# Picks transposed some steps later, and two weight splits held behind the second norm's scaling

## The chip, the cores and the metric

One core of a Trainium2 chip. The metric is the device time of one execution in microseconds; less is better.

## The reference

One decoder block on x of 256 tokens x 1024 (batch 1), all in float32. It has two residual steps. In the first, RMSNorm(x) times one wide matrix gives the inputs of an attention branch (16 heads, here one causal block of 256 keys) and of a Mamba-2 branch (convolution, scan, gated norm); both are projected to 1024, gated, summed and multiplied by `w_out`. The second is a retrieval of experts, cut here to what matters:

```
xn = rms_norm(x, norm2_g)
q  = (xn @ w_q).reshape(T, 8, 256)
s1 = einsum('thd,hkd->thk', q[..., :128], keys1)
s2 = einsum('thd,hkd->thk', q[..., 128:], keys2)
v1, i1 = top_k(s1, 16)
v2, i2 = top_k(s2, 16)
sv, pos = top_k(v1[..., :, None] + v2[..., None, :], 16)
eidx = take_along_axis(i1 * 128 + i2, pos)
gw = softmax(sv)
act = einsum('td,thkd->thk', xn, u_tab[eidx])
x = x + einsum('thk,thkd->td', gelu(act) * gw, v_tab[eidx])
```

## The kernel before

**Weights.** All weights pass through one stream of 392 pieces of 128 x 1024 float32: 88 of the input projection, 24 of the two branch projections, 8 of `w_out` (112 to 119), 16 of `w_q` (120 to 135), 128 of `u_tab` and 128 of `v_tab`. A piece is loaded on SP's queue (L107, a ring `wr` of three buffers) and split into two float32r parts, `wh` by an ACT copy (L120, ring of four) and `wl` = raw - `wh` by a subtraction (ring of four) on DVE (L128), or, for about a third of the pieces, on POOL (L125). `ahead()` (L110) keeps loads five and splits three pieces ahead of the one in use; `state["cap"]` limits the splits. Every product is three matmuls: high x high, high x low, low x high.

**Order.** The kernel is written as a main line of matmuls, with the small work as Python generators in `active`. `tick()` (L141) advances each of them by one `yield`. In `product_T` (L155) and `u_pair` (L906) a tick comes after every 12 matmuls, in `product_half` (L177) after every 12 too. The framework then orders the instructions of each engine itself, by its own estimated costs and the program's order as priority, so an engine's order can differ from the written one. `tc.issue_after(ins)` makes what is issued within it follow `ins` on the same engine. `tc.keep_in_program_order` does so for the engine's previous instruction. Each engine runs its queue in order.

**Second norm.** After the input stage the out projection makes four blocks `b` of 256 columns into the PSUM tiles `pO` (L730 to L741). For blocks 2 and 3 it makes the first token half (`tt` = 0), appends `norm2(0)`, and then the second half with `norm2(1)`. `norm2` (L721) adds the residual into `xt` (L713), sums squares (L718), adds them (L724), takes the root on POOL (`rn`, L198), scales `xt` into `xn` (L238, two instructions of 512 columns), has `xn` transposed on TensorE (L243), and ACT and DVE make `xh` (L250) and `xl` (L251) of it. `psq0` (L743) is the first block of the queries: its first token half needs `xh` and `xl` of the first half alone. Its weights are pieces 120 and 121. Piece 120's `wl` is a DVE subtraction, piece 121's a POOL one; those of 122 and 123 are already put behind the last `xh` and `xl` (L118). Before the change the splits of 120 and 121 are issued while the weights of blocks 2 and 3 are fetched.

**Picks.** `topk(tt)` (L811) finds the 16 experts of 8 heads for one token half in 61 steps on DVE: top 16 of the scores, of the candidates, softmax weights, then for each of two key halves a one-hot over ranks that yields the index `so` (L864 to L881). The step after the second `so` transposes both `so` and the weights `gt` on TensorE into the PSUM tile `ptk` (L885), and the next step copies them to `selT` (ACT, L887) and `g2` (DVE, L890 to L892). `picks` (L959) chains topk(0) and topk(1), and `paced` puts each step's DVE work behind the last `wl`.

**u_tab and gates.** `u_pair` (L906) multiplies xn with two pieces of `u_tab` in 48 matmuls. After the pair in which `picks` ends, `start` is set (L969), the pool of the picks is closed, and `one_hots` (L929) and `gate_group` (L942) of 8 tokens each follow over the remaining pairs: with n = 62 - `start`, pair k after it has the groups from 32k/n to 32(k+1)/n. Then the `v_tab` stage makes the output.

Of the kernel before, what the change touches and what calls it, by code (L numbers as in the profile page):

```python
# [15 lines left out]
OP = mybir.AluOpType  # L16
# [45 lines left out]
def tile_hybrid_block(ctx: ExitStack, tc: tile.TileContext, x, n1g, wblk, wdt, qkg, cw, cb, dtb,  # L62
# [3 lines left out]
    V = nc.vector  # L66
# [9 lines left out]
    xt = const.tile([128, 2, D], F32, name="xt")  # L76
# [3 lines left out]
    def K(ins):  # L80

        return tc.keep_in_program_order(ins) if state["start"] else ins

    def f32(ap):
        return ap.bitcast(F32)


    srcs = []
# [12 lines left out]
    state = dict(next=0, loaded=0, split=0, behind=None, start=True)  # L101
    LOAD_AHEAD, SPLIT_AHEAD = 5, 3

    def load_raw():
        i = state["loaded"]
        raw[i] = ring.tile([128, 1024], F32, name=f"wr{i}", tag="wr", bufs=3)
        nc.sync.dma_start(raw[i], srcs[i])  # L107
        state["loaded"] += 1

    def ahead():  # L110
        while state["loaded"] < min(len(srcs), state["next"] + LOAD_AHEAD):
            load_raw()
        while state["split"] < min(len(srcs), state["next"] + SPLIT_AHEAD, state.get("cap", len(srcs))):
            i = state["split"]
            r = raw.pop(i)
            h = ring.tile([128, 1024], F32R, name=f"wh{i}", tag="wh")
            lo = ring.tile([128, 1024], F32R, name=f"wl{i}", tag="wl")
            behind = state["behind"] if 122 <= i < 124 else None  # L118
            with tc.issue_after(behind[0].ins) if behind else nullcontext():
                K(A.activation(h, r, AF.Copy))  # L120
            if i == 0:
                nc.gpsimd.tensor_tensor(lo[:, :512], r[:, :512], f32(h)[:, :512], op=OP.subtract)
                state["rest"] = lo[:, 512:], r[:, 512:], f32(h)[:, 512:]
            elif i in (1, 121) or (2 < i < n_u + 128 and not 116 <= i < 124 and i % (3 if i >= 88 else 4) == PS[i >= 88]):
                state["pool"] = nc.gpsimd.tensor_tensor(lo, r, f32(h), op=OP.subtract)  # L125
            else:
                with tc.issue_after(behind[1].ins) if behind else nullcontext():
                    state["wl"] = K(V.tensor_tensor(lo, r, f32(h), op=OP.subtract))  # L128
            parts[i] = (h, lo)
            state["split"] += 1  # L130

    def next_w():
        i = state["next"]
        ahead()
        state["next"] += 1
        h, lo = parts.pop(i)
        return h, lo

    active = []

    def tick():  # L141

        for it in list(active):
            if next(it, "end") == "end":
                active.remove(it)
# [24 lines left out]
    def natural_w():  # L170
        w = []
        for f in range(2):
            h, lo = next_w()
            w += [(h[:, 256 * c:256 * c + 256], lo[:, 256 * c:256 * c + 256]) for c in range(4)]
        return w
# [28 lines left out]
    def ps_tile(tag, name):  # L204
        return psum.tile([128, 512], F32, name=name, tag=tag, bufs={"mm": 3, "tr": 2, "at": 3}[tag])

    with tc.tile_pool(name="pa", bufs=1) as pa, ExitStack() as ctx2:
# [20 lines left out]
        def norm_T(pool, tt, ss, gain, dh, dl, tag, row=False):  # L228

            r = rstd_of(pool, ss, 1, 1.0 / D, "rn")  # L230
            yield
            t = slice(128 * tt, 128 * tt + 128)
            pts = []
            for f in range(2):
                xn = pool.tile([128, 512], F32, name="xn", tag="w512", bufs=W512)
                c = slice(512 * f, 512 * f + 512)
                if row:
                    V.scalar_tensor_tensor(xn, xt[:, tt, c], r, gain[:, c], op0=OP.mult, op1=OP.mult)  # L238
                else:
                    K(V.tensor_scalar(xn, xt[:, tt, c], r, None, op0=OP.mult))  # L240
                pt = ps_tile(tag, "ptx").rearrange("p (c t) -> p c t", c=4)
                for c in range(4):
                    nc.tensor.transpose(pt[:, c], xn[:, 128 * c:128 * c + 128], ident)  # L243
                pts.append(pt)
            yield
            for f in range(2):
                if row:
                    k = slice(4 * f, 4 * f + 4)
                    state["behind"] = (
                        A.activation(dh[:, k, t], pts[f], AF.Copy),  # L250
                        V.tensor_tensor(dl[:, k, t], pts[f], f32(dh[:, k, t]), op=OP.subtract))  # L251
                else:
                    for c in range(4):
                        k = 4 * f + c
                        K(A.activation(dh[:, k, t], pts[f][:, c], AF.Copy, scale=gain[:, k:k + 1]))
                    for c in range(4):
                        k = 4 * f + c
                        state["behind"] = K(
                            V.scalar_tensor_tensor(dl[:, k, t], pts[f][:, c], gain[:, k:k + 1], f32(dh[:, k, t]),
                                                   op0=OP.mult, op1=OP.subtract))  # L260
                yield
# [67 lines left out]
        def half(t):  # L329
            return t.rearrange("p (a n) -> p a n", a=2)  # L330
# [362 lines left out]
        for b in range(4):  # L693
# [11 lines left out]
                                   op0=OP.mult, op1=OP.subtract)  # L705
# [24 lines left out]
        for b in range(2):  # L730
            po = half(ps_tile("mm", "pO"))
            product_N(po, mh, ml)
            for tt in range(2):
                residual(b, tt, po)
        po = {b: half(ps_tile("mm", "pO")) for b in (2, 3)}
        w = {b: natural_w() for b in (2, 3)}
        state["cap"] = 122
        for tt in range(2):
            for b in po:
                product_half(po[b], tt, w[b], mh, ml)  # L740
            active.append(norm2(tt, po))  # L741

        psq0 = half(ps_tile("mm", "psq"))  # L743
        w = natural_w()
        first = len(active) > 1 and active[0]
        while first in active:
# [64 lines left out]
    def topk(tt):  # L811
# [20 lines left out]
        gt = tk.tile([128, 8, 16], F32, name="gt", tag="gt")  # L832
# [30 lines left out]
        sel = []  # L863
        for f in range(2):  # L864

            xf = tk.tile([128, 8, 16, 2], F16, name="xf", tag="xf")
            V.tensor_copy(xf, idx[:, tt, :, f][:, :, :, None].to_broadcast([128, 8, 16, 2]))
            eq = pb.tile([128, 8, 16, 16], F16, name="eq", tag="oh", bufs=2)
            V.tensor_tensor(eq, ranks[:, f][:, :, None, :].to_broadcast([128, 8, 16, 16]),
                            it16[:, None].to_broadcast([128, 8, 16, 16]), op=OP.is_equal)  # L870
            yield
            e8 = eq.rearrange("p h r (k e) -> p (h r) k e", e=2)
            V.tensor_tensor(e8, e8, xf.rearrange("p h r e -> p (h r) e")[:, :, None, :]
                            .to_broadcast([128, 128, 8, 2]), op=OP.mult)
            yield
            for n in (8, 4, 2):
                V.tensor_tensor(eq[:, :, :n], eq[:, :, :n], eq[:, :, n:2 * n], op=OP.add)
            so = tk.tile([128, 8, 16], F32, name="so", tag="so", bufs=4)
            V.tensor_tensor(so, eq[:, :, 0], eq[:, :, 1], op=OP.add)
            sel.append(so)  # L880
            yield  # L881
        t = slice(128 * tt, 128 * tt + 128)
        pt = ps_tile("tr", "ptk").rearrange("p (a t) -> p a t", a=4)
        for i, src in enumerate((sel[0], sel[1], gt)):
            nc.tensor.transpose(pt[:, i], src.rearrange("p h k -> p (h k)"), ident)  # L885
        yield
        A.activation(selT[:, 16 * tt:16 * tt + 16].rearrange("p q f e -> p f q e"),  # L887
# [2 lines left out]
        V.tensor_scalar(gf, pt[:, 2], GS, None, op0=OP.mult)  # L890
        V.tensor_copy(g2[:, 0, t], gf)
        V.tensor_tensor(g2[:, 1, t], gf, g2[:, 0, t], op=OP.subtract)  # L892
        yield

    done = dict(t=0)

    def halves(a, b):

# [60 lines left out]
    picks = paced(itertools.chain(topk(0), topk(1)))  # L959
# [6 lines left out]
    start = None  # L966
    for jp in range(64):
        u_pair(jp)
        if start is None and (picks not in active or jp >= 30):  # L969
            while picks in active:  # L970
                tick()
            tkctx.close()
            pb2 = ctx.enter_context(tc.tile_pool(name="pb2", bufs=1))
            gA[1] = pb2.tile([128, 64, T], F32, name="gA1")
            start = jp
            one_hots(0)
        elif start is not None:
            n = 62 - start
            k = jp - start - 1
            if k < n:  # L980
                for q in range(32 * k // n, 32 * (k + 1) // n):
                    gate_group(q, 2 * jp + 2)
                    if q + 1 < 32:
                        one_hots(q + 1)
# [3 lines left out]
    for jp in range(64):  # L988
# [16 lines left out]
        for r in range(8):  # L1005
            jj, tt, n = (r // 4, r // 2 % 2, r % 2) if jp < 63 else (r % 2, r // 4, r // 2 % 2)
            o = py[2 * tt + n]
            product(jj, tt, slice(512 * n, 512 * n + 512), o)
            if jp == 63 and jj == 1:
                m = 256 if r == 7 else 512  # L1010
                for p in range(512 // m):
                    c = slice(512 * n + m * p, 512 * n + m * p + m)
# [68 lines left out]
```

## Time and profile before

| | us |
|---|---|
| median of 3 runs | 1261.83 (1261.42 to 1262.97) |
| the profiled execution | 1262.0 |
| its span, first to last instruction | 1260.3 |
| TensorE busy | 1234.1 |
| VectorE (DVE) busy | 895.8 |
| ScalarE (ACT) busy | 634.5 |
| GpSimd (POOL) busy | 291.5 |

In the rows below PE is TensorE's matmuls, PEld its weight loads, SP the queue that issues loads. An arrow reads output <- inputs by the names of the program. The mean granted clock of TensorE over the span is 0.989 of full. Times in rows with a start are microseconds from the span's start.

### The profile page before, as it was taken

The numbers are of one execution on the slowest core, as the hardware profiler recorded it, in microseconds if no ns is written. First come the engines' busy times: TensorE is split into PE (matmuls) and PEld (weight loads), VectorE is DVE, ScalarE is ACT, GpSimd is POOL, SyncE is SP. The second block draws the span as 40 slices with busy tenths as digits, with TensorE's granted clock in tenths as the row PEclk, the third lists the DMA queues.
The fourth block names the chain that finished last, engine by engine and source line by source line (L and its number), as shares of the span: only waits on it lengthen the run. The fifth ranks groups of instructions, "written<-read, shape, count | busy, mean of one in ns | idle before, by whom it ended". The sixth has DMA issues, their size and how long they took to land.

```text
span 1260.3 us, 22718 instructions
## 1 busy us (share of the span) xinstructions
PE 1234.1 (98%) x9005; PEld 1147.5 (91%) x9005; DVE 895.8 (71%) x1582; ACT 634.5 (50%) x978; POOL 291.5 (23%) x160
## 2 busy tenths in 40 slices
PE   7999999999999999989989999999999999999998
PEld 6989989999999899989989999999988888888887
DVE  5888989898344666687686888999855555555554
ACT  4666665666434355444544444444444444544443
POOL 3355453444223122222322222222100000000000
PEclk8999999999999999989989999999999999999999
DMA  5534444534555455545544444444455555555553
GB/s 186 175 134 160 159 168 151 168 134 151 176 195 181 151 192 163 182 151 178 175 153 163 159 162 166 153 152 167 168 190 194 199 186 199 187 197 196 189 197 119
DMA packets 60345, 215.15 MB, mean 171 GB/s; under 512 B 7600, under 2 KB 8144, under 8 KB 60112
## 3 DMA queue, kind: packets, MB, share of 16 engines
q1 hardware_dynamic: 60240, 213.71, 50.1%
q8 instruction: 70, 1.15, 0.4%
q14 instruction: 35, 0.29, 0.1%
HBM read 212.60 MB, written 1.08 MB: 170 GB/s over the span
## 4 chain that ended last, share of the span: by engine, by line
PE 88%; DVE 8%; POOL 2%; ACT 1%; issue 1%; DMA 1%; SPq 0%; DVEq 0%; POOLq 0%
PE py L1001 9%; PE py L1000 9%; PE py L1002 9%; PE psu L913 9%; PE psu L914 9%; PE psu L915 9%; PE psqk L185 3%; PE psg L951 2%; PE psv L185 2%; PE pO L185 2%; PE psz L185 2%; POOL p L471 1%; DVE wl L128 1%; DVE acc L526 1%; PE pS L165 1%; PE pS L166 1%
## 5 line engine op out<-in xcount | busy, mean ns | idle before, releaser
L120 ACT ACTIVATE wh<-wr 128x1024 fp32r<-128x1024 f32 x392 | 413.7, 1056 | 352.1 <-PE psu L914 110.1
L128 DVE TENSOR_TENSOR wl<-wr,wh 128x1024 fp32r<-128x1024 f32 x312 | 382.8, 1228 | 218.4 <-ACT wh L120 217.1
L125 POOL TENSOR_TENSOR wl<-wr,wh 128x1024 fp32r<-128x1024 f32 x79 | 199.3, 2523 | 436.6 <-ACT wh L120 388.6
L913 PE MATMUL psu<-xh,wh 128*128 128x256 f32 x1024 | 294.7, 288 | 0.0
L915 PE MATMUL psu<-xh,wl 128*128 128x256 f32 x1024 | 291.8, 285 | 0.0
L914 PE MATMUL psu<-xl,wh 128*128 128x256 f32 x1024 | 291.7, 285 | 0.0
L1000 PE MATMUL py<-wh,hh 128*128 128x512 f32 x512 | 199.2, 389 | 0.0
L1001 PE MATMUL py<-wl,hh 128*128 128x512 f32 x512 | 199.2, 389 | 0.0
L1002 PE MATMUL py<-wh,hl 128*128 128x512 f32 x512 | 199.2, 389 | 0.0
L914 PEld LDWEIGHTS psu<-xl,wh 128*128 128x128 f32 x1024 | 198.7, 194 | 0.0
L915 PEld LDWEIGHTS psu<-xh,wl 128*128 128x128 f32 x1024 | 198.6, 194 | 0.0
L913 PEld LDWEIGHTS psu<-xh,wh 128*128 128x128 f32 x1024 | 198.6, 194 | 0.0
L1000 PEld LDWEIGHTS py<-wh,hh 128*128 128x128 f32 x512 | 96.1, 188 | 20.1
L1002 PEld LDWEIGHTS py<-wh,hl 128*128 128x128 f32 x512 | 96.1, 188 | 19.9
L1001 PEld LDWEIGHTS py<-wl,hh 128*128 128x128 f32 x512 | 96.1, 188 | 19.8
L992 ACT ACTIVATE hh<-gA 128x512 fp32r<-128x512 f32 x64 | 40.4, 632 | 88.9 <-PE py L1001 88.8
L993 DVE SCALAR_TENSOR_TENSOR hl<-gA,hh 128x512 fp32r<-128x512 f32 x64 | 44.4, 693 | 52.4 <-ACT hh L992 52.4
L938 DVE TENSOR_TENSOR og<-oh,g 128x1024 f16<-128x1024 f16 x64 | 54.7, 891 | 0.9
L526 DVE SCALAR_TENSOR_TENSOR acc<-u,cws,acc 128x254 f32<-128x254 f32 (+2 forms) x96 | 51.1, 564 | 0.5 <-ACT acc L522 0.4
L956 ACT ACTIVATE gA<-psg 128x32 f32<-128x32 f32 (+27 forms) x72 | 18.8, 281 | 63.5 <-DVE gA L954 54.0
L471 POOL TENSOR_SCALAR p<-p,rs 128x128 f32<-128x128 f32 (+1 forms) x32 | 41.1, 1300 | 38.5 <-DVE rs L469 38.5
L954 DVE TENSOR_TENSOR gA<-gA,psg 128x256 f32<-128x256 f32 (+11 forms) x118 | 37.4, 352 | 10.8 <-PE psg L951 10.5
(320 smaller groups left out, 2420.8 us busy)
## 6 DMA issues: line engine op xcount, KB each, us to landing
wr<-in_u_tab SPq DMA_DIRECT2D x128, 512.0 KB, 3.3
wr<-in_v_tab SPq DMA_DIRECT2D x128, 512.0 KB, 3.2
wr<-in_wblk SPq DMA_DIRECT2D x88, 512.0 KB, 3.3
wr<-in_wso SPq DMA_DIRECT2D x16, 512.0 KB, 4.1
wr<-in_wpq SPq DMA_DIRECT2D x16, 512.0 KB, 3.9
ar<-acT SPq DMA_DIRECT2D x8, 512.0 KB, 3.9
wr<-in_wao SPq DMA_DIRECT2D x8, 512.0 KB, 3.3
wr<-in_wou SPq DMA_DIRECT2D x8, 512.0 KB, 3.3
```

The costliest lines, as they stand in the source:

```text
L120: K(A.activation(h, r, AF.Copy))
L125: state["pool"] = nc.gpsimd.tensor_tensor(lo, r, f32(h), op=OP.subtract)
L128: state["wl"] = K(V.tensor_tensor(lo, r, f32(h), op=OP.subtract))
L185: mm(ps[:, tt], lhs[:, k, s], rhs, start=f == n == 0, stop=f == 1 and n == 11)
L526: V.scalar_tensor_tensor(acc[:, i, sh:], u[:, i, :T - sh], cws[:, ct, 3 - sh:4 - sh], acc[:, i, sh:], op0=OP.mult, op1=OP.add)
L913: mm(ps[:, jj], h[:, c], xh[:, c], start=c == 0, stop=False)
L914: mm(ps[:, jj], h[:, c], xl[:, c], start=False, stop=False)
L915: mm(ps[:, jj], lo[:, c], xh[:, c], start=False, stop=c == 7)
L938: V.tensor_tensor(og[:, i], oh[:, 1], g2[:, i, t].rearrange("p (g e) -> p g e", e=2)[:, :, None, :] .to_broadcast([128, 4, 128, 2]), op=OP ...
L1000: mm(o, hh[:, jj, s], h[:, c], start=j == 0, stop=False)
L1001: mm(o, hh[:, jj, s], lo[:, c], start=False, stop=False)
L1002: mm(o, hl[:, jj, s], h[:, c], start=False, stop=j == 127)
```

## The change

`topk` no longer transposes its picks: its last step appends a generator `turned_picks` to `active`, which takes five empty steps and then does what topk did; a counter `done["picks"]` tells the loop over u_tab when both are through. In the second norm, the first token half gets one empty step more after the root; the cap is 120 while blocks 2 and 3 fetch weights and 122 only from the fetch of `psq0`'s; piece 120's DVE split follows the last `xn` issued so far, and piece 121's POOL split waits for that `xn`.

```diff
+    def after(ins, other):
+        tc.add_manual_dep(ins.ins, other.ins.name,
+                          mybir.DependencyInfo(mybir.DependencyClass.Sync, mybir.DependencyReason.DATA), reason="after")
+        return ins
...
             behind = state["behind"] if 122 <= i < 124 else None
-            with tc.issue_after(behind[0].ins) if behind else nullcontext():
+            if 120 <= i < 122:
+                behind = None, state["xn"]
+            with tc.issue_after(behind[0].ins) if behind and behind[0] else nullcontext():
                 K(A.activation(h, r, AF.Copy))
...
                 state["pool"] = nc.gpsimd.tensor_tensor(lo, r, f32(h), op=OP.subtract)
+                if behind:
+                    after(state["pool"], behind[1])
             else:
                 with tc.issue_after(behind[1].ins) if behind else nullcontext():
                     state["wl"] = K(V.tensor_tensor(lo, r, f32(h), op=OP.subtract))
...
             r = rstd_of(pool, ss, 1, 1.0 / D, "rn")
             yield
+            if row and tt == 0:
+                yield
...
-                    V.scalar_tensor_tensor(xn, xt[:, tt, c], r, gain[:, c], op0=OP.mult, op1=OP.mult)
+                    state["xn"] = V.scalar_tensor_tensor(xn, xt[:, tt, c], r, gain[:, c], op0=OP.mult, op1=OP.mult)
...
         po = {b: half(ps_tile("mm", "pO")) for b in (2, 3)}
+        state["cap"] = 120
         w = {b: natural_w() for b in (2, 3)}
-        state["cap"] = 122
         for tt in range(2):
...
         psq0 = half(ps_tile("mm", "psq"))
+        state["cap"] = 122
         w = natural_w()
...
             sel.append(so)
             yield
+        active.append(turned_picks(tt, (sel[0], sel[1], gt)))
+
+    def turned_picks(tt, srcs):
+
+        for _ in range(5):
+            yield
         t = slice(128 * tt, 128 * tt + 128)
         pt = ps_tile("tr", "ptk").rearrange("p (a t) -> p a t", a=4)
-        for i, src in enumerate((sel[0], sel[1], gt)):
+        for i, src in enumerate(srcs):
             nc.tensor.transpose(pt[:, i], src.rearrange("p h k -> p (h k)"), ident)
         yield
...
+        done["picks"] += 1
+        yield
+
+    done = dict(t=0, picks=0)
...
-        if start is None and (picks not in active or jp >= 30):
-            while picks in active:
+        if start is None and (done["picks"] == 2 or jp >= 30):
+            while done["picks"] < 2:
                 tick()
```

## Rows read from the trace of the kernel before

**Rows 1.** The page, part 1: busy us (share of the span) and instructions.
```profile
PE 1234.1 (98%) x9005; PEld 1147.5 (91%) x9005; DVE 895.8 (71%) x1582; ACT 634.5 (50%) x978; POOL 291.5 (23%) x160
```

**Rows 2.** Waits of PE: who waited for whom, us in total, times, longest us.
```profile
PE ptk L885 <- DVE so L879: 7.5, 2, 3.9
```

**Rows 3.** PE in order of time, first wait: start us, us [idle before <-releaser].
```profile
550.82 0.27 PE L885 MATMUL ptk<-ident,so 128*128 128x128 f32 x1
555.01 0.48 PE L885 MATMUL ptk<-ident,so 128*128 128x128 f32 x1 [3.91 <-DVE so L879]
...
555.35 0.56 PE L913 MATMUL psu<-xh,wh 128*128 128x256 f32 x1
...
560.62 0.31 PE L913 MATMUL psu<-xh,wh 128*128 128x256 f32 x1
```

**Rows 4.** The same view, second wait.
```profile
648.47 0.28 PE L885 MATMUL ptk<-ident,so 128*128 128x128 f32 x1
...
650.13 0.28 PE L914 MATMUL psu<-xl,wh 128*128 128x256 f32 x1
653.97 0.48 PE L885 MATMUL ptk<-ident,so 128*128 128x128 f32 x1 [3.56 <-DVE so L879]
...
659.58 0.32 PE L915 MATMUL psu<-xh,wl 128*128 128x256 f32 x1
```

**Rows 5.** Stretches: length, busy PE PEld DVE ACT POOL, granted clock, DMA share, GB/s.
```profile
536.00:551.00 15.00, 15.00 (x126) 14.86 (x125) 14.59 (x21) 8.23 (x10) 3.53 (x2) 1.00 0.51 175
...
554.00:556.00 2.00, 0.99 (x5) 0.99 (x6) 1.88 (x9) 0.26 (x1) 0.34 (x1) 0.50 0.52 168
...
562.00:635.00 73.00, 73.00 (x610) 73.00 (x610) 49.67 (x208) 36.02 (x41) 19.25 (x8) 1.00 0.54 181
...
672.00:900.00 228.00, 228.00 (x2139) 226.71 (x2138) 203.09 (x283) 107.39 (x207) 60.41 (x23) 1.00 0.48 160
...
437.00:441.00 4.00, 4.00 (x22) 3.53 (x21) 2.96 (x9) 1.20 (x2) 0.56 (x1) 0.60 0.38 131
```

**Rows 6.** DVE in order of time before the two waits.
```profile
554.69 0.27 DVE L879 TENSOR_TENSOR so<-eq 128x128 f32<-128x128 f16 x1
...
649.02 1.21 DVE L933 TENSOR_TENSOR oh<-iot,selT 128x2048 f16<-128x2048 f16 x1
...
653.64 0.28 DVE L879 TENSOR_TENSOR so<-eq 128x128 f32<-128x128 f16 x1
```

**Rows 7.** The page, part 5: busy us, mean ns | idle before, releaser.
```profile
L120 ACT ACTIVATE wh<-wr 128x1024 fp32r<-128x1024 f32 x392 | 413.7, 1056 | 352.1 <-PE psu L914 110.1
L128 DVE TENSOR_TENSOR wl<-wr,wh 128x1024 fp32r<-128x1024 f32 x312 | 382.8, 1228 | 218.4 <-ACT wh L120 217.1
```

**Rows 8.** DVE in order of time at the second norm.
```profile
431.30 1.22 DVE L128 TENSOR_TENSOR wl<-wr,wh 128x1024 fp32r<-128x1024 f32 x1
...
433.83 3.49 DVE L238 SCALAR_TENSOR_TENSOR xn<-xt,rn,tg 128x512 f32<-128x512 f32 x2 [0.45 <-POOL rn L198]
...
438.64 0.41 DVE L718 SCALAR_TENSOR_TENSOR sqo<-xt 128x256 f32<-128x256 f32 x1
...
440.59 1.42 DVE L238 SCALAR_TENSOR_TENSOR xn<-xt,rn,tg 128x512 f32<-128x512 f32 x2 [0.67 <-POOL rn L198]
```

**Rows 9.** POOL in order of time at the second norm.
```profile
433.76 2.34 POOL L125 TENSOR_TENSOR wl<-wr,wh 128x1024 fp32r<-128x1024 f32 x1
```

**Rows 10.** PE in order of time at the second norm.
```profile
436.71 0.66 PE L243 MATMUL ptx<-ident,xn 128*128 128x128 f32 x4 [2.49 <-DVE xn L238]
...
438.05 0.58 PE L185 MATMUL psq<-wh,xh 128*128 128x256 f32 x1
...
444.10 0.39 PE L185 MATMUL psq<-wh,xl 128*128 128x256 f32 x1 [0.22 <-DVE xl L251]
```

More of the change, by code (lines that the diff above doesn't have):

```diff
@@ L892, in topk @@
         V.tensor_tensor(g2[:, 1, t], gf, g2[:, 0, t], op=OP.subtract)
+        done["picks"] += 1
         yield
-    done = dict(t=0)
+    done = dict(t=0, picks=0)
     def halves(a, b):
```

## The prediction

> **What bounds the kernel now.** I read the page first. TensorE is busy for 98% of the span [rows 1], so time comes back only where TensorE stands still or runs slowly. Next I asked which waits TensorE itself has. The largest is for the picks: the three transposes `ptk` of each token half wait for `so`, in two waits that add up to 7.5 us, the longest 3.9 us [rows 2]. Then I read TensorE's instructions around both waits in order of time. In the first, a transpose starts at 550.82, the next one at 555.01, and the matmuls behind them then run 24 starts in 5.27 us (555.35 to 560.62), 0.22 us apiece [rows 3]. The undisturbed pace is 610 instructions in 73 us, 0.12 us apiece, at a granted clock of 1.00; in the stretch behind the wait the granted clock is 0.50, the lower of the two levels, 1.2 GHz [rows 5]. So a wait is paid twice: as standing time and as slow matmuls after it. The second wait is the same picture [rows 4]. The third place is the second norm: there TensorE stands 2.49 us for `xn`, and the granted clock of the four microseconds after it is 0.60 [rows 5, 10].
>
> **The transposes of the picks.** Nothing is removed: three transposes, the ACT copy into `selT` and three small DVE operations per token half stay. They move to a chain of their own that sits out five steps. A step is one `tick`, issued after every 12 matmuls, so 12 x 0.12 = 1.44 us. Formerly the transposes came in the step after the last `so`; now that step appends the new chain, its first turn is one step later, and five of its turns are empty: six steps, 8.6 us. Meanwhile TensorE works on the u_tab matmuls that stood behind the transposes.
>
> Is `so` ready by then? It ends at 554.69 + 0.27 = 554.96 [rows 6]. The transposes' new place is 550.82 + 8.6 = 559.5, so 4.5 us are to spare. topk(1) begins two steps earlier than now, because it no longer sits behind the transposes; if three of its pieces (under 1 us each) come ahead of `so`, 2 us are left. In the second half `so` ends at 653.92, and it has 1.21 us of one-hots (and the `og` behind them) ahead of it [rows 6], which then come later. Its place moves six steps back against a start two steps earlier, so four later, 5.8 us against a wait of 3.6 [rows 4].
>
> What comes back, first half: from 550.82 to 560.62 is 9.80 us; it holds three transposes and 24 matmuls, which at 0.12 are 3.24 us. That is 6.56 us. Second half: from 650.13 to 659.58 is 9.45 us; it holds one matmul, two transposes and 24 matmuls, 3.24 us, so 6.21 us. Sum: **-12.8 us**. Only the standing time, 7.5 us, would be the lower bound, if the clock fell for a reason other than the wait.
>
> What is late next? DVE is full ahead of each wait (14.59 of 15 us [rows 5]), and so far the wait let it catch up. Without it DVE carries a lag of some 4 us on, and the weight splits `wl` stand in the same queue. They have room: a split can begin when a buffer of the ring of four comes free, three weights before its use, 3 x 24 x 0.12 = 8.6 us; less 1.06 us for ACT's copy and 1.23 for DVE's [rows 7] that is 6.3 us, more than the lag. From 562 on DVE is busy 49.67 of 73 us [rows 5], so a lag of 4 us is gone after some 12 us. I cost this at nothing; if the room is exceeded, TensorE waits at each weight (the last rival). The end of the picks, and with it the first one-hots, comes one pair of u_tab blocks later; the 32 gate groups then lie in 35 pairs, not 36. Their work is the same. DVE is busy 203.09 of 228 us there [rows 5]; 36/35 of that is 92%, still under full. Cost nothing; ACT only waits later for the same transposes.
>
> **The splits beside the second norm.** Weights 120 and 121 are split in the same number of operations, but the DVE split goes behind the last `xn` of the first token half, and the POOL split waits for it; an empty step more for the first half moves the transposes of `xn` in the program. Now the DVE split (431.30, 1.22 us) runs ahead of the sum of squares' last steps, and the POOL split (433.76 to 436.10) covers the first `xn`: the two `xn` of this half take 3.49 us, those of the other half 1.42 [rows 8, 9]. Without both, the first half's `xn` start 1.1 us sooner, at 432.7, and end at 432.7 + 1.42 = 434.1 rather than 437.3, about when the out projection's matmuls run out, so the 2.49 us go down to 0 to 0.5; with eight transposes at 0.12 the first query matmuls can start near 435.2, not 438.05 [rows 10].
>
> But little of that reaches the end, as the second half's chain follows: squares, root on POOL, `xn`, transposes, `xh`, `xl`. It takes from 438.64 [rows 8] to 444.10 [rows 10], 5.46 us, and 24 matmuls of the first half (2.9 us) can't fill it. Queued behind the held splits are, on DVE, the residual, `xl` and the squares of the second half, and on POOL its root. The POOL split now runs from 434.1 (or, behind the DVE split, 435.2) to 436.5 or 437.5. Best case: the squares start at 435.3 as soon as the projection ends, 3.3 us sooner. Middle: they start at 437.5, 1.1 us sooner. Worst: the planned order puts the second half's transposes ahead of up to 16 first-half matmuls that could have run, 1.9 us, so about 1 us lost. I take **-1.5 us**, between the middle and the best, since the DVE order can also put the `xl` behind the squares and shorten the chain. The loads of weights 123 and 124 wait for the ring's buffers, so for these splits; they come some 3 us later on SP's queue and the key load behind them too, but ACT splits those weights only after the second half's `xh`.
>
> Here a rule weighs in. The row: an `xn` beside a POOL split takes 2.1 us more than the others [rows 8, 9]. The Trainium skill, "SBUF — State Buffer", section "Who interferes with whom", says that a DVE instruction with two SBUF inputs and a GpSimd instruction that reads SBUF exclude each other for the whole instruction, and that issue order decides who blocks. By that rule the trace's long `xn` agrees, and the change doesn't remove the conflict but moves it to the next such DVE instruction. With the row alone the sum stays as below; by the rule it is that of rival B.
>
> **Sum.** The profiled run took 1262.0 us, 0.2 above the median of the three runs. 1262.0 - 12.8 - 1.5 = 1247.7; less 0.2 for the median: **1247.5 us**.
>
> **Rivals.**
> A, as forecast: both waits for the picks gone, the norm worth 0 to -3.3: 1245.7 to 1249. Chance 0.75.
> B, the block moves: the POOL split, released by `xn`, runs while the second half's squares want to (`xt` twice from SBUF, 0.41 us [rows 8]) and its root queues behind it on POOL; TensorE then stands where the first half's matmuls run out, and the slow clock with it. The norm costs 0 to 2.5 us instead (the present wait again): 1249 to 1251.5. For it: the 2.1 us that the blocked `xn` lost; against: 24 matmuls lie in between. Chance 0.13. This is what the skill's rule named above would do.
> C, one half's `so` is still late by its six steps: one of the two gains is lost, 1253.7 to 1255. For it: 4.5 us of margin are not many beside DVE's lag. Chance 0.06.
> D, it doesn't do what it says: the order on TensorE is planned by estimated times, and if these let the transposes up again, or DVE's topk(1) pushes `so` back just as far, all stays: 1260 to 1263. Against: the first transposes stand at their place in the program, right at a step's end [rows 3]. Chance 0.03.
> E, slower: without the catch-up DVE becomes the bound between 551 and 650. From a lag of 6.3 us on, each weight makes TensorE wait; over 34 weights 0.5 us each is 17 us, which eats the 14.3 and ends at 1264.6. It needs 3.4 us of DVE per weight of 2.88 us; it has 49.67/73 x 2.88 = 1.96 [rows 5]. Chance 0.03.
>
> **Numbers.** The range takes A and B whole and C where the norm is at its best (1261.8 - 6.2 - 3.3 = 1252.3), with a little under A for the unknown order on TensorE: 1245.0 to 1253.5. The rest of C, D and E, about 0.1, is left out. What a measurement of this kernel can tell is about 0.2%, 2.5 us; A, B and C are all more than that below 1261.83, so faster 0.94, same 0.03 (D), slower 0.03 (E).
>
> **What would show it.** Right: no wait of TensorE for `so`; granted clock 1.00 from 545 to 660; the transposes in the profile six steps after the place where they now stand; the four `xn` at some 0.75 us each; the POOL split starting after the second of them; the first query matmul 2 to 3 us earlier. Wrong: a wait for `so` or `wl` among TensorE's waits, a slow stretch of clock after 545, DVE busy near 100% from 562 on, or a wait for the second half's `xn` that is longer than the present 2.49 us.

## The result, and the profile after

The changed kernel takes 1246.78 us (median of 4 runs, 1246.62 to 1247.01), the kernel before 1261.62 us beside it (median of 4 runs, 1258.15 to 1262.97). The ratio is 0.9886, with a 95% interval of 0.9874 to 0.9897: 1.1% faster. Forecast were 1247.5 us and 1245.0 to 1253.5; it is the case called A there.

The profiled run took 1246.86 us, its span is 1244.8 us, 15.5 us under that of before. Part 1 of the page after, busy time and share of the span:

```profile
PE 1228.4 (99%) x9005; PEld 1140.7 (92%) x9005; DVE 897.4 (72%) x1583; ACT 633.9 (51%) x975; POOL 296.0 (24%) x160
```

TensorE's largest waits after (us in total, times, longest). The wait for `so` [rows 2] is not among them, and that for the second norm's `xn`, now line 250, has shrunk from 2.5 us to two of 0.9 and 0.2:

```profile
PE psqk L195 <- DVE hTl L271: 1.5, 1, 1.5
PE pty L651 <- DVE y L646: 1.5, 2, 1.2
PE pz L282 <- DVE zb L279: 1.3, 1, 1.3
...
PE ptx L255 <- DVE xn L250: 1.1, 2, 0.9
```

DVE after, in order of time, at the last `so` of each token half (answers to [rows 6]):

```profile
551.95 0.27 DVE L892 TENSOR_TENSOR so<-eq 128x128 f32<-128x128 f16 x1
...
641.73 0.29 DVE L892 TENSOR_TENSOR so<-eq 128x128 f32<-128x128 f16 x1
```

TensorE after, at the transposes of the two halves (answers to [rows 3, 4]); both groups run without an idle time in front:

```profile
556.65 0.38 PE L904 MATMUL ptk<-ident,so 128*128 128x128 f32 x2
556.87 0.27 PE L904 MATMUL ptk<-ident,gt 128*128 128x128 f32 x1
...
645.02 0.38 PE L904 MATMUL ptk<-ident,so 128*128 128x128 f32 x2
645.24 0.27 PE L904 MATMUL ptk<-ident,gt 128*128 128x128 f32 x1
```

So `so` is ready 556.65 - 552.22 = 4.43 us ahead in the first half and 645.02 - 642.02 = 3.0 us in the second. The stretch around both, TensorE alone (length, busy, granted clock, DMA share, GB/s), is filled to the last hundredth at full clock; in the kernel before the same stretch has 107.53 us at 0.94:

```profile
545.00:660.00 115.00, 115.00 (x962) 1.00 0.53 180
```

The second norm after, on DVE (answers to [rows 8]):

```profile
429.53 0.42 DVE L725 TENSOR_TENSOR xt<-xt,pO 128x256 f32<-128x256 f32 x1 [1.00 <-PE pO L195]
...
431.88 1.42 DVE L250 SCALAR_TENSOR_TENSOR xn<-xt,rn,tg 128x512 f32<-128x512 f32 x2 [0.67 <-POOL rn L208]
433.21 1.22 DVE L138 TENSOR_TENSOR wl<-wr,wh 128x1024 fp32r<-128x1024 f32 x1
434.35 1.28 DVE L263 TENSOR_TENSOR xl<-ptx,xh 128x512 fp32r<-128x512 f32 x2
435.55 0.75 DVE L725 TENSOR_TENSOR xt<-xt,pO 128x256 f32<-128x256 f32 x2
436.21 0.78 DVE L730 SCALAR_TENSOR_TENSOR sqo<-xt 128x256 f32<-128x256 f32 x1
...
436.92 0.42 DVE L730 SCALAR_TENSOR_TENSOR sqo<-xt 128x256 f32<-128x256 f32 x1
...
438.39 1.42 DVE L250 SCALAR_TENSOR_TENSOR xn<-xt,rn,tg 128x512 f32<-128x512 f32 x2 [0.67 <-POOL rn L208]
```

On POOL (answers to [rows 9]), the split of weight 121:

```profile
433.53 3.17 POOL L133 TENSOR_TENSOR wl<-wr,wh 128x1024 fp32r<-128x1024 f32 x1 [1.68 <-DVE xn L250]
```

And on TensorE (answers to [rows 10]): the transposes of the first half, its first query matmul, the transposes of the second half, and the second half's third query matmul, the first one that needs `xl`:

```profile
432.69 1.32 PE L255 MATMUL ptx<-ident,xn 128*128 128x128 f32 x8 [0.20 <-DVE xn L250]
...
435.26 0.28 PE L195 MATMUL psq<-wh,xh 128*128 128x256 f32 x1
...
439.20 1.32 PE L255 MATMUL ptx<-ident,xn 128*128 128x128 f32 x8 [0.87 <-DVE xn L250]
...
441.27 0.39 PE L195 MATMUL psq<-wh,xl 128*128 128x256 f32 x1 [0.22 <-DVE xl L263]
```

Where the 15.5 us went, from the two traces. Between the start of the first half's last residual (430.08 before, 429.53 after) and that third query matmul (444.10 [rows 10], 441.27), TensorE has the same work in both; the interval falls from 14.02 to 11.74 us, **2.28 us**. From there to the end of the span 1260.3 - 444.10 = 816.2 us become 1244.8 - 441.27 = 803.5: **12.7 us**, the picks. The 0.55 us ahead of the norm lie where nothing was changed; below they swing by as much from kernel to kernel.

### The profile page after: what moved, and what is told of

Its sections match the earlier page's. It is cut to its first block, busy times and chain, and to the rows that moved or that the text cites. A ratio compares the mean times of both kernels' runs of the same rounds, so it can differ in the third digit from the quotient of the medians.

```text
span 1244.8 us, 22716 instructions
## 1 busy us (share of the span) xinstructions
PE 1228.4 (99%) x9005; PEld 1140.7 (92%) x9005; DVE 897.4 (72%) x1583; ACT 633.9 (51%) x975; POOL 296.0 (24%) x160
## 4 chain that ended last, share of the span: by engine, by line
PE 90%; DVE 6%; POOL 2%; issue 0%; DMA 0%; SPq 0%; ACT 0%; DVEq 0%; POOLq 0%
PE psu L933 10%; PE psu L935 10%; PE psu L934 10%; PE py L1020 9%; PE py L1022 9%; PE py L1021 9%; PE psqk L195 3%; PE psg L971 2%; PE psv L195 2%; PE psz L195 2%; PE pO L195 2%; POOL p L483 1%; DVE acc L538 1%; PE pS L175 1%; PE pS L176 1%; PE pS L174 1%
## 5 line engine op out<-in xcount | busy, mean ns | idle before, releaser
L133 POOL TENSOR_TENSOR wl<-wr,wh 128x1024 fp32r<-128x1024 f32 x79 | 204.0, 2583 | 421.4 <-ACT wh L128 355.3
L958 DVE TENSOR_TENSOR og<-oh,g 128x1024 f16<-128x1024 f16 x64 | 58.5, 952 | 1.0
L976 ACT ACTIVATE gA<-psg 128x24 f32<-128x24 f32 (+28 forms) x70 | 18.6, 281 | 64.4 <-DVE gA L974 55.2
L974 DVE TENSOR_TENSOR gA<-gA,psg 128x256 f32<-128x256 f32 (+12 forms) x120 | 38.1, 352 | 10.2 <-PE psg L971 9.8
```

Of the source, the lines that this page charges most:

```text
L958: V.tensor_tensor(og[:, i], oh[:, 1], g2[:, i, t].rearrange("p (g e) -> p g e", e=2)[:, :, None, :] .to_broadcast([128, 4, 128, 2]), op=OP ...
```

## The experiments

Each kernel is told as an edit of the changed one. "Norm interval" is the interval just used; it does not depend on what lies ahead of it.

**1. The picks alone.** The norm part of the change is taken back:

```diff
-            if 120 <= i < 122:
-                behind = None, state["xn"]
...
-                if behind:
-                    after(state["pool"], behind[1])
...
-            if row and tt == 0:
-                yield
...
-        state["cap"] = 120
         w = {b: natural_w() for b in (2, 3)}
+        state["cap"] = 122
```

> The new chain of the picks alone; the second norm as before. My theory (both waits for the picks are gone, with the slow clock behind them, 12.8 us; the norm's part is separate): 1248.9 us, no wait of TensorE for so, and at the second norm the wait of 2.49 us and the slow stretch behind it as before. Rival (most of the gain comes from the norm, or the parts only work together): 1255 us or more.

Measured 1249.37 us (1249.28 to 1250.13), ratio 0.9909 (0.9892 to 0.9926), close to the theory's 1248.9 and far from the rival's 1255. The old wait for `xn` stands alone at the head of TensorE's waits (us in total, times, longest), and the norm interval is 13.99:

```profile
PE ptx L249 <- DVE xn L244: 2.5, 1, 2.5
```

**2. The norm alone.** The picks part is taken back:

```diff
-        active.append(turned_picks(tt, (sel[0], sel[1], gt)))
-
-    def turned_picks(tt, srcs):
-
-        for _ in range(5):
-            yield
...
-        if start is None and (done["picks"] == 2 or jp >= 30):
-            while done["picks"] < 2:
+        if start is None and (picks not in active or jp >= 30):
+            while picks in active:
```

> The held splits, the caps and the empty step at the second norm alone; the picks as before. My theory: the third query matmul of the second token half comes 2.3 us sooner against the matmuls before the norm, so 1259.4 us, with both waits for so still there, 3.9 and 3.6 us. Rival (the 2.3 us are lost again in the next wait): 1261.7 us.

Measured 1257.35 us (1255.93 to 1259.92), ratio 0.9975 (0.9964 to 0.9986). The waits for `so` are what they were, to the digit [rows 2], while the norm interval is the changed kernel's 11.74:

```profile
PE ptk L898 <- DVE so L892: 7.5, 2, 3.9
```

It is 2.0 us under the expectation, and the stretches say where to look. TensorE of the kernel before, windows behind the first wait, continuing [rows 5] (length, busy, granted clock, DMA share, GB/s):

```profile
556.00:558.00 2.00, 2.00 (x11) 0.50 0.44 174
558.00:560.00 2.00, 2.00 (x12) 0.50 0.00 0
560.00:562.00 2.00, 2.00 (x16) 0.83 0.21 45
```

The same behind the first wait of this kernel, where the transpose is let go at 551.91:

```profile
552.00:554.00 2.00, 2.00 (x10) 0.50 0.80 258
554.00:556.00 2.00, 2.00 (x15) 0.78 0.01 4
556.00:558.00 2.00, 2.00 (x19) 1.00 0.00 0
```

The wait is the same 3.9 us, but the low clock lasts to about 561 there, six microseconds behind the transpose, and to about 555 here, three microseconds behind it. So the price of a wait is no constant. The other runs point the same way: of the 15 runs of the kernel before that belong to this experiment, the seven with a mean granted clock of 0.989 took 1261.9 to 1262.9 us, the seven with 0.992 or 0.993 took 1258.5 to 1261.2. Both kernels with these waits spread over 4 us from run to run (1258.5 to 1262.9 in 15 runs, 1255.9 to 1259.9 in 10). But kernel 3 below, with two waits as well, spreads over 1.4 in six runs, and the changed kernel, without them, over 0.4 in the four runs of the result and over 2.2 in kernel 12.

**3 and 4. How many empty steps the picks need.** None, and then (with `range(2)`) two, instead of five:

```diff
-        for _ in range(5):
+        for _ in range(0):
```

> The changed kernel with no empty step in the picks' chain, so that the transposes come five steps, 7.2 us, sooner. In the changed kernel they start 4.4 us after so is ready in the first half and 3.1 us after it in the second; so they would now wait 2.8 and 4.1 us. My theory (a wait is paid as standing time and again as slow matmuls, 2.3 us each): 1246.8 + 6.9 + 4.6 = 1258 us. Rival 1 (only the standing time counts): 1253.7 us. Rival 2 (the gain came from topk(1) starting two steps sooner and the one-hots later, not from the place of the transposes): 1247 us.

Measured 1257.32 us (1256.34 to 1257.71), ratio 0.9969 (0.9956 to 0.9981). TensorE waits for `so` again:

```profile
PE ptk L904 <- DVE so L892: 6.7, 2, 4.2
```

This kernel is 10.5 us slower than the changed one, of which it stands 6.7; the other 3.8 us are matmuls at the low clock (granted 0.50 from 554 to 556 and from 646 to 650). That is the theory's outcome, not one of the rivals': with the chain of its own but without empty steps the kernel is as slow as kernel 2, which has no such chain.

> The changed kernel with two empty steps instead of five: the transposes come 4.3 us sooner. First half: just about when so is ready, no wait or a few tenths. Second half: a wait of about 1.2 us. If a wait of that length also lowers the clock: 1246.8 + 1.2 + 2.3 = 1250.3 us and a granted clock of 0.50 behind it; if it is too short for that: 1248.0 us and a clock of 1.00.

Measured 1247.86 us (1247.65 to 1248.11), ratio 0.9896 (0.9879 to 0.9913). One wait is left, in the second half:

```profile
PE ptk L904 <- DVE so L892: 1.1, 1, 1.1
```

and the clock of the stretch does not fall for it:

```profile
545.00:660.00 115.00, 113.90 (x956) 1.00 0.56 179
```

So this kernel loses 1.1 us between the medians for 1.1 us of standing: this short wait is paid once.

**5. POOL's split free, DVE's held.**

```diff
-                if behind:
-                    after(state["pool"], behind[1])
```

> The changed kernel without the POOL split's wait for the last xn; the DVE split is still held. The order of instructions on each engine stays. Theory (DVE operations with two SBUF inputs and a POOL split exclude each other for the whole instruction): the split of weight 121 then starts as soon as its ACT copy is there, some 2 us earlier, beside the second xn or the DVE split of weight 120; one of these takes 2 to 3.3 us instead of 0.75 or 1.22, and what stands behind it on DVE (xl, residual, squares) is late by as much, so the second half's query matmuls come up to 2 us later: 1247.5 to 1249. Rival (holding the DVE split alone brings the gain): the POOL split takes its time where nobody waits, 1246.8 within 0.4.

Measured 1249.26 us (1249.12 to 1249.75), ratio 0.9908 (0.9887 to 0.9929), just above the theory's range; the norm interval is 13.58 us. In order of time on DVE, POOL and TensorE:

```profile
433.76 3.41 DVE L136 TENSOR_TENSOR wl<-wr,wh 128x1024 fp32r<-128x1024 f32 x1
...
433.45 2.64 POOL L133 TENSOR_TENSOR wl<-wr,wh 128x1024 fp32r<-128x1024 f32 x1 [1.05 <-issue]
...
437.23 0.38 PE L193 MATMUL psq<-wl,xh 128*128 128x256 f32 x1 [1.12 <-DVE wl L136]
```

POOL's split begins 0.3 us ahead of DVE's, which then takes 3.41 us instead of 1.22, and the query matmuls wait for it. What the hold buys is the order of these two: with it DVE's split begins first (433.21) and POOL's, at 433.53, waits instead (3.17 us), where nobody needs it yet.

**6. DVE's split free, POOL's held.**

```diff
-                with tc.issue_after(behind[1].ins) if behind else nullcontext():
+                with tc.issue_after(behind[1].ins) if behind and behind[0] else nullcontext():
                     state["wl"] = K(V.tensor_tensor(lo, r, f32(h), op=OP.subtract))
```

> The changed kernel without the hold on the DVE split of weight 120; the POOL split still waits for the last xn. Theory (the DVE split ahead of the norm's last steps costs its own time on the path): xn starts about 1.2 us later than in the changed kernel, TensorE's wait for the first half's xn is about 1 us longer, and the end comes 0.5 to 1.5 us later: 1247.3 to 1248.3. Rival (the second half's chain alone decides, and it has room): 1246.8 within 0.4.

Measured 1247.97 us (1247.43 to 1248.11), ratio 0.9895 (0.9875 to 0.9916); the norm interval is 12.48 us. DVE's split runs ahead of the root once more, so the `xn` start 3.75 us behind the first half's last residual instead of 2.35. TensorE's wait for them does not grow by 1 us, as the theory had it, but only from 0.20 to 0.42; the time is lost in the second half. In turn POOL's split meets no split on DVE (2.38 us), but a square of the second half, which takes 1.57 instead of 0.42:

```profile
431.26 1.22 DVE L138 TENSOR_TENSOR wl<-wr,wh 128x1024 fp32r<-128x1024 f32 x1
...
436.53 1.57 DVE L730 SCALAR_TENSOR_TENSOR sqo<-xt 128x256 f32<-128x256 f32 x1
...
435.43 2.38 POOL L133 TENSOR_TENSOR wl<-wr,wh 128x1024 fp32r<-128x1024 f32 x1 [1.68 <-DVE xn L250]
```

**7. Both splits on DVE.**

```diff
-            elif i in (1, 121) or (2 < i < n_u + 128 and not 116 <= i < 124 and i % (3 if i >= 88 else 4) == PS[i >= 88]):
+            elif i == 1 or (2 < i < n_u + 128 and not 116 <= i < 124 and i % (3 if i >= 88 else 4) == PS[i >= 88]):
```

> The changed kernel with the split of weight 121 on DVE instead of POOL, so that POOL runs no split beside the norm at all. If the POOL split still costs the second half (its 3.17 us, the blocked square of 0.78 instead of 0.42), this gives 0.3 to 1 us back: 1245.8 to 1246.5. If it costs nothing where it is now, the added 1.22 us of DVE work between the second half's steps is on the path: 1247.3 to 1248.3.

Measured 1247.46 us (1247.08 to 1249.94), ratio 0.9898 (0.9875 to 0.9922); norm interval 12.51 us, 0.77 more. Taking POOL out of the norm ends every blocking there, and still costs more than it gives, because 1.22 us of DVE work come into the chain: TensorE's wait for the second half's `xn` grows from 0.87 to 1.67 us.

**8. Without the extra empty step of the first half.**

```diff
-            if row and tt == 0:
-                yield
```

> The changed kernel without the norm's extra empty step for the first half. Theory: the step only sets where the eight transposes stand in TensorE's queue; without it they stand earlier among the out projection's matmuls, so TensorE waits longer for xn and has these matmuls left for later, where it would have waited too: 1246.8 within 0.5. Rival (the transposes' place decides): the wait for the first xn grows by as many matmuls as stand behind it, 12 at 0.12 us, 1.4 us: 1248.2.

Measured 1247.13 us (1246.53 to 1247.19), ratio 0.9888 (0.9867 to 0.9909); norm interval 11.73 us. The step does nothing that these runs can tell.

**9. No split of the u_tab weights on POOL.** The rival that DVE becomes the bound, pushed:

```diff
-            elif i in (1, 121) or (2 < i < n_u + 128 and not 116 <= i < 124 and i % (3 if i >= 88 else 4) == PS[i >= 88]):
+            elif i in (1, 121) or (2 < i < n_u and not 116 <= i < 124 and i % (3 if i >= 88 else 4) == PS[i >= 88]):
```

> The changed kernel with every split of the u_tab weights on DVE, none on POOL: 15 splits more on DVE between 545 and 672 us and 22 more from 672 to 900, 1.22 us each. In the changed kernel DVE is busy 103.25 of 127 us in the first stretch and 202.31 of 228 in the second. If DVE was near its bound (rival E of the prediction), the second stretch needs 202.3 + 26.8 = 229 us of 228 and the first 121.6 of 127, so TensorE waits for wl and the end comes 2 to 12 us later: 1249 to 1259. If DVE has more room than its busy share says, because part of that share is waiting behind POOL's splits (which then ends), TensorE sees nothing: 1246.8 within 0.5, with DVE below 97% in the second stretch.

Measured 1246.38 us (1245.74 to 1247.46), ratio 0.9887 (0.9870 to 0.9903). DVE in the two stretches, first of the changed kernel (length, busy, granted clock, DMA share, GB/s):

```profile
545.00:672.00 127.00, 103.25 (x283) 1.00 0.54 183
672.00:900.00 228.00, 202.31 (x286) 1.00 0.47 159
```

then of this one, with 15 and 22 splits more on DVE:

```profile
545.00:672.00 127.00, 107.90 (x295) 1.00 0.57 183
672.00:900.00 228.00, 197.74 (x307) 1.00 0.50 160
```

In the second stretch DVE does 22 splits more and is busy 4.6 us less. Two groups from 672 to 900 show why (busy us, mean ns of one, idle before and its releaser). The changed kernel:

```profile
L138 DVE TENSOR_TENSOR wl<-wr,wh 128x1024 fp32r<-128x1024 f32 x48 | 58.6, 1220 | 12.4 <-ACT wh L128 11.8
L958 DVE TENSOR_TENSOR og<-oh,g 128x1024 f16<-128x1024 f16 x57 | 50.0, 917 | 0.9
```

This kernel:

```profile
L138 DVE TENSOR_TENSOR wl<-wr,wh 128x1024 fp32r<-128x1024 f32 x70 | 85.6, 1223 | 16.1 <-ACT wh L128 12.6
L958 DVE TENSOR_TENSOR og<-oh,g 128x1024 f16<-128x1024 f16 x56 | 36.4, 689 | 0.9
```

The splits add 27.0 us, yet the sum falls, because the other operations get shorter: one `og` takes 689 ns where it took 917. DVE's "busy" holds time in which an operation stood blocked behind a split on POOL, and when the split is gone it comes back.

**10. The second half's squares on ACT.** Suggested by the blocked square of 0.78 us and by ACT, which has nothing to do from 434.6 to 439.9:

```diff
-            if b < 2:
+            if b < 2 or tt == 1:
                 A.activation(sq, xt[:, tt, s], AF.Square, accum_out=ss4[:, tt, b:b + 1])
```

> The changed kernel with the two squares of the second half's norm on ACT instead of DVE (the same sums of squares); ACT stands from 434.6 to 439.9 us there. Theory (the second half's chain on DVE sets when its query matmuls start, and the POOL split delays its first square): the chain from the residual to the root is shorter by the blocked square and one more, 0.78 + 0.42, less one square of ACT and its handing over, some 0.6 us: gain 0.4 to 0.8 us, 1246.0 to 1246.4. Rival (the chain has room there): 1246.8 within 0.2.

Measured 1245.78 us (1245.02 to 1246.24), ratio 0.9880 (0.9864 to 0.9896). The norm interval is 11.37 us, 0.37 under the changed kernel and just under the expected 0.4, and TensorE's wait for the second half's `xn` 0.49 instead of 0.87:

```profile
438.14 1.32 PE L255 MATMUL ptx<-ident,xn 128*128 128x128 f32 x8 [0.49 <-DVE xn L250]
```

Of the 1.1 us between the spans of the two traces (1243.7 against 1244.8) only the 0.37 is the edit's; 0.7 us lie ahead of the norm (the first half's last residual starts at 428.83 instead of 429.53), in code that is the same. It has the lowest median of the study, but by less than its runs spread.

**11. And POOL's split of weight 121 behind the second half's `xn`.** Kernel 10, and the split put off:

```diff
-                state["pool"] = nc.gpsimd.tensor_tensor(lo, r, f32(h), op=OP.subtract)
-                if behind:
-                    after(state["pool"], behind[1])
+                if behind:
+                    state["late"] = lo, r, f32(h)
+                else:
+                    state["pool"] = nc.gpsimd.tensor_tensor(lo, r, f32(h), op=OP.subtract)
...
+            if row and tt == 1:
+                state["pool"] = after(nc.gpsimd.tensor_tensor(*state.pop("late"), op=OP.subtract), state["xn"])
             yield
```

> The one before, with POOL's split of weight 121 issued behind the second half's last xn instead of the first half's, so that no split on POOL stands beside either chain. If what is left of the exclusion costs anything once the squares are on ACT (the second root behind the split on POOL, a blocked residual), up to 0.4 us more than the one before: 1245.7 to 1246.2. If not, the same as the one before within 0.2; if the split comes too late for the key product, TensorE waits for wl there and it is 0.5 to 2 us slower.

Measured 1250.98 us (1249.44 to 1252.85), ratio 0.9922 (0.9907 to 0.9938). The split comes too late, and more is lost than the expectation allowed: TensorE has two waits close together,

```profile
439.87 1.32 PE L256 MATMUL ptx<-ident,xn 128*128 128x128 f32 x8 [1.85 <-DVE xn L251]
...
443.12 0.58 PE L196 MATMUL psq<-wl,xh 128*128 128x256 f32 x1 [1.94 <-POOL wl L259]
443.50 0.41 PE L196 MATMUL psq<-wh,xl 128*128 128x256 f32 x1
```

and the next 24 matmuls start 0.21 us apart (443.50 to 448.41), at the low clock (granted 0.50 from 442 to 448). The second half's third query matmul starts at 446.06, so the norm interval is 15.49 us, 4.1 more than in kernel 10.

**12. The changed kernel once more.**

> The changed kernel once more, nothing edited, to see how far its own time and the part ahead of the second norm move from one set of runs to another. In the kernels so far the last residual of the norm's first half began between 428.83 and 430.10 us, and from there to the third query matmul of the second half every kernel with the same orders took 11.73 or 11.74. If the medians of the experiments differ by what their norm takes and otherwise by this part only, the time is 1246.0 to 1247.3, the interval 11.74 again; if the changed kernel repeats within 0.2 of 1246.8, the differences of half a microsecond between the experiments are their own.

Measured 1247.01 us (1245.46 to 1247.61), ratio 0.9883 (0.9867 to 0.9900); norm interval 441.41 - 429.67 = 11.74 us. The median moved by 0.23 us and the four runs spread over 2.2, so half a microsecond between two medians says little here; the norm interval repeats to a hundredth, and the experiments on the norm are read by it. In kernel 11 the first half's last residual starts at 430.57, outside the span of times given in the expectation.

The norm's parts by that interval:

| kernel | last residual of the first half starts | third query matmul | interval |
|---|---|---|---|
| POOL's split put off, squares on ACT (11) | 430.57 | 446.06 | 15.49 |
| before | 430.08 | 444.10 | 14.02 |
| picks alone (1) | 429.76 | 443.75 | 13.99 |
| POOL's split free (5) | 430.07 | 443.65 | 13.58 |
| both splits on DVE (7) | 429.27 | 441.78 | 12.51 |
| DVE's split free (6) | 430.04 | 442.52 | 12.48 |
| norm alone (2) | 429.24 | 440.98 | 11.74 |
| changed | 429.53 | 441.27 | 11.74 |
| without the extra step (8) | 430.10 | 441.83 | 11.73 |
| squares on ACT (10) | 428.83 | 440.20 | 11.37 |

Kernels 3, 4 and 9, whose norm is that of the changed kernel, take 11.74 us as well. The hold on POOL's split is worth 13.58 - 11.74 = 1.84 us of the 2.28, the hold on DVE's 0.74. They don't add up, since either alone leaves a long blocking in the chain (3.41 us in kernel 5, 1.57 in kernel 6). What the two caps do without the holds was not run.

## Why the prediction was right, and where it was off

**The transposes of the picks: right, -12.8 said, 12.7 in the profiles.** The place came out as worked out: six steps of 1.44 us are 8.6 us. Ahead of the picks the changed trace is 0.55 + 2.28 = 2.83 us early, so the old place is at 550.82 - 2.83 = 547.99, and the transposes start at 556.65, 8.66 us behind it. The margin of `so` was said to be 4.5 us and is 4.43; for the second half 5.8 - 3.6 = 2.2 were left and 3.0 are there. So the pieces of topk(1) that could have come ahead of `so`, and would have left 2 us, cost it nothing. That a wait is paid twice is shown by kernel 3: 6.7 us of standing, 10.5 us of loss. But the term was taken from one execution with long low-clock stretches as if every run had them. Between medians the picks are worth 1261.52 - 1249.37 = 12.15 us (kernel 1 against the kernel before, on one chip) or 1257.35 - 1246.78 = 10.6 (kernel 2 against the changed one, the norm's part in both). The traces say the same when read from the third query matmul to the end of the span, which leaves out the norm and what lies ahead of it: 816.2 us in the kernel before and 814.0 in kernel 2, where kernel 1 takes 803.6 and the changed kernel 803.5: differences of 12.6 and 10.5. So 12.8 is the top of what was found, not the middle. What makes the low clock last three microseconds in one execution and six in another stays open.

**DVE's lag: right that it costs nothing.** No wait for `wl` is among TensorE's larger ones, and the stretch from 545 to 660 has none at all. DVE is busier behind the picks: 56.65 us of the 73 from 562 to 635, where it had 49.67 [rows 5], though the work in this stretch is not quite the same, since the changed kernel is ahead. From 672 to 900 it is busy 202.31 of 228 us (203.09 before). DVE is further from being the bound there than the prediction put it, which took the 203.09 for work and made it 92%: kernel 9 puts 37 more splits on DVE and loses nothing, since part of that share was standing behind POOL's splits.

**The second norm: right in sign and place, too small, -1.5 said, 2.28 measured.** Right: four `xn` at 0.71 us each (1.42 for two), POOL's split behind the second of them, the first query matmul at 435.26 instead of 438.05, so 2.8 us earlier as the traces stand and 2.24 when the 0.55 ahead of the norm is taken off. Two steps failed.

The first is the sentence that the second half's chain takes 5.46 us from its squares to the third query matmul and follows as it was. The square at 438.64 from which this is counted [rows 8] is the last of the half's two. Before, the first of them had run ahead of the `xn`, and an `xl` stood between the last one and the sum. On DVE before:

```profile
432.95 0.42 DVE L718 SCALAR_TENSOR_TENSOR sqo<-xt 128x256 f32<-128x256 f32 x1
...
438.98 0.69 DVE L251 TENSOR_TENSOR xl<-ptx,xh 128x512 fp32r<-128x512 f32 x1
```

After, both `xl` run ahead of both squares, and from the last square the chain takes 441.27 - 436.92 = 4.35 us, 1.11 less. Of these, 0.48 lie between that square and `xn` (440.59 - 438.64 = 1.95 before, 438.39 - 436.92 = 1.47 after), where the `xl` is gone; the prediction hoped for a shorter chain from the opposite order, `xl` behind the squares. The other 0.63 lie behind the start of `xn` (444.10 - 440.59 = 3.51 before, 441.27 - 438.39 = 2.88 after), because before TensorE itself was late: after its 2.49 us of standing it took 4.04 us for 20 query matmuls (438.05 to 442.09), 0.20 apiece instead of 0.12 (granted 0.50 from 438 to 440), and reached the second half's transposes 1.50 us behind the start of `xn`; after, they start 0.81 us behind it, at a clock of 1.00. So the prediction applied "paid twice" to both picks and forgot it at the norm.

The second is the bound for the squares: 1.1 us sooner if they wait for POOL's split, 3.3 if not, and 1.5 taken. Like for like, the last square starts at 436.92 instead of 438.64, which is 1.17 us sooner when the 0.55 is taken off. The best case was out of reach even without POOL: the projection's last matmul starts at 435.14, and behind it two residuals (435.55, 0.75 us) and a second square come first. POOL's split, which ran until 436.70, held up one square, to 0.78 us, but neither the `xl` nor the residuals (1.28 and 0.75 us for two; 0.68 for one and 0.74 for two in kernel 7, where POOL has no split): these read one operand from PSUM. The root, which rival B saw queue behind the split, starts 1.10 us after its end. This is rival B's mechanism at work, but at a price of 0.36 us, where rival B let it eat the norm's whole gain and up to 2.5 us more. The Trainium skill, "SBUF — State Buffer", section "Who interferes with whom", gives the rule in both halves: a DVE instruction with two operands from SBUF contends with a GpSimd instruction that reads SBUF, one with at most one (outside the 2-port modes) does not, and the order of issue decides who blocks. The changed kernel and kernels 5, 6 and 9 agree with it (0.78 instead of 0.42 us beside an `xl` that keeps its time, 3.41 instead of 1.22, 1.57 instead of 0.42, 917 instead of 689 ns). Kernel 5 shows how near the worse case was: with POOL's split 0.3 us ahead of DVE's, four fifths of the norm's gain are gone.

So the 2.28 us are 1.17 from the earlier squares and 1.11 from the shorter chain. The 1.5 was 0.3 too much for the first and left out nearly all of the second; that it came within 0.8 us of the sum is in part luck.

**The sum.** 12.8 + 1.5 = 14.3 us were said; the profiled runs differ by 15.1, the medians by 14.8. In the profiles the error is the norm's 0.8 us and the 0.55 ahead of it, less 0.1 at the picks and 0.4 that lie outside the spans (1262.0 - 1260.3 = 1.7 us before, 1246.86 - 1244.8 = 2.06 after). In the medians an overstated first term and an understated second one (1249.37 - 1246.78 = 2.6 us for the norm) hide each other in part, so the sum is nearer than its terms.

## What to carry to other kernels

Where the engine that sets the time waits in its own queue for something that will be ready soon, move the waiting instruction behind work that is ready: two of the five empty steps brought nearly all of it here, and the rest bought the last 1.1 us and some margin. Price such a wait by its standing time and the slow matmuls behind it, at every place where it stands, and expect the second part to differ from run to run. Before two engines that exclude each other are set to work beside a chain, ask which one starts first: a hold that makes the one nobody waits for start second was worth more here than taking the work off POOL (kernel 7).

## What the runs showed of the hardware

- The granted clock of TensorE: waits of 1.1 us (kernel 4) and 1.67 us (kernel 7) left it at 1.00, one of 2.49 us was followed by 0.50 (kernel before, at the norm), and two of 1.85 and 1.94 us close together were too (kernel 11). Behind two waits of the same 3.9 us it stayed at 0.50 for some six microseconds in one execution and three in another.
- DVE's busy time is not all work: with 22 splits fewer on POOL and 22 more on DVE it fell from 202.31 to 197.74 us of 228 (kernel 9).
- The part ahead of the norm, the same code in all kernels, moved the start of the first half's last residual between 428.83 (kernel 10) and 430.57 us (kernel 11).
